# A decoder trunk on one core: unread matmuls at the start, cache pages loaded by fours, the first half's last rows two products sooner

## The chip, the cores and the metric

The kernel runs on one core of one Trainium2 chip. The metric is the device time of one execution in microseconds; a kernel's time is the median of its runs. The kernel before took 1762.97 us (three runs, 1758.93 to 1764.65).

## The reference, cut to what matters

Two layers of a decoder trunk work on 544 tokens: one prompt of 512 and eight samples of four, each sample with 256 tokens of cached past that lie in pages of 128 rows. All is float32. The parts that the change touches:

```python
def rmsnorm(x, g):
    return x * rsqrt(mean(x * x, axis=-1) + 1e-6) * g

h = rmsnorm(x, g_in[l])
z = h @ w_in[l]          # 1024 -> queries, 6 kv streams, gates, conv, pool, ...
# k_cmp, v_cmp (no rotary): rows of the cached pages and of the prompt,
# in overlapping blocks of 32 tokens (stride 16), through a small MLP:
def compress_blocks(rows, pe, w1, w2):
    blk = rows[:, idx] + pe
    return gelu(blk @ w1) @ w2
# compressed attention + top-k selected blocks + sliding window,
# each head's three branches weighted by sigmoid gates (z's 24 gate columns)
...
x = x + merged @ w_out[l]
x = x + ((silu(causal_dwconv3(h2 @ W_a)) * (h2 @ W_b)) @ W_down)   # h2 = rmsnorm(x)
# after the last layer: y = rmsnorm(x, norm_final)
```

## The kernel before

**Products.** Activations lie with features on partitions: eight tiles of 128 x 544, worked in two halves of 272 columns. Weights and activations are split in a high part, rounded to the type that TensorE takes at full rate, and a low part, the rest. A product turns 1024 features into 128: for each of two halves and eight 128-feature slices `mm3` (L321) issues three matmuls, high weights by high activations (L323), high by low (L324) and low by high (L326), 48 in all. A weight tile is loaded by SyncE's queue (SP, L306) as 512 KB into one of three raw buffers; ACT casts it to the high part (L298), DVE subtracts it for the low part (L299), each in two pieces of 128 x 512. The gate product zng has 24 columns; its high and low weights are stacked in one tile (`stacked_weights`: load L313, POOL fill L316, ACT cast L317, DVE subtraction L318).

**Order.** A list of tasks (`tasks`) names the products of a layer. It begins with zkc, zvc, zks (products 0 to 2, run together in the norm group, so that the first layer can start before all of x is normalised), zkw (3), zq0 to zq3 (4 to 7), zvs (8), zvw (9), zng (10), then a convolution product, two pieces of the compression MLP on the key pages, a convolution product, and two pieces on the value pages. `emit` issues a product's matmuls; before that `take` calls `ahead`, which issues weight loads up to three products further on (look=3), and then the task's `pre` is called, if there is one. Within the norm group the `pre` of the second and third product is called just before that product's results are taken out of PSUM. What shall follow a given number of products later is put in a list by `later` and called by `tick` after each product (or, in the last stage, half product).

PE's order is the order of the program. The other engines' instructions are ordered by the framework's scheduler on a simulated timeline, except in the setup, where ACT's and SP's are in program order too. Each engine runs its list in order, and waits on semaphores.

**Pages.** `pages_some` (L450) reads a page's number from a small table into a register of SP (`page`, L443), and issues two loads of 64 KB (L455), one for the key and one for the value rows; they arrive as runs of 256 bytes. 16 pages a layer make 32 loads into two tiles. They are started as `pre` of products: three each ahead of zks, zkw, zq0, zq1 and zq2, and the last one ahead of zq3. `cmp_split` (L525), the `pre` of the first MLP piece, casts the complete tile in eight slices of 128 x 326 (ACT, L532) into one high tile and subtracts (DVE, L534) into eight tiles of the T pool.

The same SP queue carries the weights, the four copies a product that swap halves for the rotary embedding (`z_rope`, L483) and stores of key and value rows (L974).

**Gates.** After zng `nsa_gates` forms the sigmoid gates (L688 to L693); two products later `nsa_rows` transposes them on PE (L700). `v_stack` transposes values on PE (L504), casts them on ACT (L509) and subtracts on DVE (L510) into T tiles; it too is called two products after its own product.

**Start.** `setup` loads x and the first weights in pieces; ACT and DVE form the parts of x (`norm_tile`: L1224 high, L1225 low). PE's first matmul comes when the first weights are cast.

**End.** The last down projection runs half after half: eight output tiles of the first half, then eight of the second, nine matmuls each in the last chunk. After each tile `final_tile` adds it to x and adds its square to a sum. When the first half's eighth tile is done, `final_sum(0)` is put off by fl[0] = 2 products and `final_rows(0)` by fl[1] = 7. `final_sum` sums the squares over partitions by matmuls with ones (L374) and forms the reciprocal root on DVE (L377 to L383); `final_rows` spreads it over partitions by PE transposes (L393), copies it by ACT (L395, L396), multiplies x by it on POOL (L1262, eight tiles for the first half) or DVE (L1264), and stores.

Of the kernel before, what the change touches and what calls it, by code (L numbers as in the profile page):

```python
# [6 lines left out]
F32 = mybir.dt.float32  # L7
F32R = mybir.dt.float32r
# [8 lines left out]
NP = 512  # L17
# [199 lines left out]
class Task:  # L217
    def __init__(self, name, evac, w, x, m, pre, mode, stage, halves, keep):
        self.name, self.evac, self.w, self.x, self.m = name, evac, w, x, m
        self.pre, self.mode, self.stage, self.halves, self.keep = pre, mode, stage, halves, keep  # L220
# [1 line left out]


class Trunk:
    def __init__(self, tc, ins, outs, ctx, slots=49, work=8, fill=1.66, look=3, lag=3, np_=4, nps=2, pm=9, ng=3, raw=3, by_pool=((0, 1, 2, 3, 4, 5, 6, 7), (1, 3, 5)), fl=(2, 7, 6, 1), ys=(4.0, 3.0, 10.0, 3.0, 3.0, 3.5)):
        self.tc, self.nc, self.i, self.o = tc, tc.nc, ins, outs
        pool = lambda name, **k: ctx.enter_context(tc.tile_pool(name=name, **k))
        self.cp = pool("cp", bufs=1)
        self.wp = pool("wp", bufs=4)
        self.bp = pool("bp", bufs=3)  # L230
        self.tp = pool("tp", bufs=slots)
        self.kp = pool("kp", bufs=work)
        self.dp = pool("dp", bufs=1, space=bass.MemoryType.DRAM)
        self.sp = pool("sp", bufs=2)
        self.ps = pool("ps", bufs=1, space=bass.MemoryType.PSUM)
        self.n = 0
        self.ng, self.raw = ng, raw
        self.by_pool, self.fl, self.ys_ = by_pool, fl, ys
        self.np_, self.nps, self.pm = np_, nps, pm
        self.fill, self.look, self.lag = fill, look, lag  # L240


    def nm(self, p):
# [155 lines left out]
    def setup(self):  # L399
        nc, i = self.nc, self.i  # L400
        self.cst = self.cp.tile([128, CS_W], F32, name="cst")
        self.norms = self.cp.tile([128, NM_W], F32, name="norms")
        self.ones = self.cp.tile([128, 2], F32, name="ones")
        self.vc = self.cp.tile([128, 256], F32R, name="vc").rearrange("p (g n) -> p g n", g=2)
        self.cT = self.cp.tile([128, 512], F32R, name="cT")
        self.ptt = self.cp.tile([1, 16], I32, name="ptt")
        self.cst1 = self.cst2 = None
        nc.vector.memset(self.ones, 1.0)
        nc.scalar.activation(self.ones[:, 1:2], self.ones[:, 0:1], AF.Tanh)
        self.x = [self.T() for _ in range(KT)]  # L410
        self.ident = self.c("ident")
        nc.gpsimd.memset(self.vc[64:128].bitcast(F32), 0.0)
        nc.gpsimd.memset(self.cT[64:128].bitcast(F32), 0.0)
        s, v, g = nc.scalar, nc.vector, nc.gpsimd
        by = ((s, None), (s, v), (g, None), (s, v), (s, v), (g, g), (s, v), (s, v))
        ap = self.tl[0].w[0]
        r = self.raw_weights(8)
        for t, a in ((self.norms, i["norms"]), (self.x[0], i["xT"][:, 0]), (r[:, 0:4], ap[:, 0:4]),
                     (self.x[1], i["xT"][:, 1]), (r[:, 4:8], ap[:, 4:8])):
            nc.sync.dma_start(t, a)  # L420
        for k in range(2, 7):
            nc.sync.dma_start(self.x[k], i["xT"][:, k])
        self.norm_tile(0, 0, "g_in")
        w = self.weight_parts(r, 0, 4)
        self.norm_tile(1, 0, "g_in")
        self.got[0] = w + self.weight_parts(r, 4, 8)
        self.nxt = 1
        for k in range(2, 7):
            self.norm_tile(k, 0, "g_in")
        for k in range(3):  # L430
            self.square_sum(self.x[k], k, *by[k])
        self.ahead(2)
        nc.sync.dma_start(self.x[7], i["xT"][:, 7])
        nc.sync.dma_start(self.cst, i["cst"])
        nc.sync.dma_start(self.ptt, i["pt"])
        for u in range(3, 7):
            self.square_sum(self.x[u], u, *by[u])
        self.norm_tile(7, 0, "g_in")
        self.square_sum(self.x[7], 7, *by[7])
# [522 lines left out]
    def tasks(self, l):  # L962
        nc, i = self.nc, self.i
# [3 lines left out]
        def add(name, evac, w, x=h, m=128, pre=None, mode=None, stage="rest", halves=(0, 1), keep=None):  # L967
            T.append(Task(f"{name}.{l}", evac, w, x, m, pre, mode, stage, halves, keep))

        def zt(m):  # L970
            return (i["w_in"][l, m], 8)

        def store(name, j, t):
            nc.sync.dma_start(self.o[name][l, j], t)  # L974
# [28 lines left out]
        def raw_kv(j):  # L1003
            def evac(ps):
                if j == 0:
                    nc.gpsimd.tensor_mul(self.cosr, self.cosr, self.r)
                    nc.gpsimd.tensor_mul(self.sinr, self.sinr, self.r)
                z = self.z_raw(ps)
                store("kvT", j, z)
                self.cmp_prompt(j, z)  # L1010
            return evac

        add("zkc", raw_kv(0), zt(0), pre=begin, mode="norm", stage="z")
        add("zvc", raw_kv(1), zt(1), stage="z")
        pages = lambda a: lambda: self.pages_some(l, range(a, min(a + 3, 16)))

        def rope_k(name, out, j, off, e0):
            def evac(ps):
                z = self.z_rope(ps)
                store(out, j, z)  # L1020
                setattr(self, name, self.k_stack(z, off))
                nc.gpsimd.tensor_copy(self.E[:, :, e0:e0 + 4], self.seq4(z))
            return evac

        add("zks", rope_k("ksel", "kvT", 2, 32, 16), zt(2), pre=pages(0), stage="z")
        add("zkw", rope_k("kwin", "wT", 0, 0, 20), zt(3), pre=pages(3), stage="z")

        def rope_q(r):
            def evac(ps):
                self.q[r] = self.z_rope(ps)  # L1030
                if r == 3:
                    self.sample_prep()
            return evac

        for r in range(4):
            add("zq", rope_q(r), zt(4 + r), pre=pages(6 + 3 * r), stage="z")

        def raw_v(name, out, j, e0):
            def evac(ps):
# [32 lines left out]
        for j in range(2):  # L1072
            for u, nme in enumerate("cxb"):
                add("zconv", conv(j, nme), zt(10 + 3 * j + u), stage="z" if j == 0 and u < 2 else "fill")
                if j == 0 and u < 2:
                    for a in range(2):
                        add("cmp", cmp(u, a), (i["cw1"][l, u][:, 8 * a:8 * a + 8], 8),
                            x=lambda a=a: self.cmpx[8 * a:8 * a + 8],
                            pre=(lambda st=u: self.cmp_split(st)) if a == 0 else None, mode=f"cmp{a}", stage="z")
# [345 lines left out]
```

## Time and profile before

| | us |
|---|---|
| median of three runs (lowest, highest) | 1762.97 (1758.93, 1764.65) |
| the profiled execution | 1759.85 |
| its span, first to last instruction | 1758.0 |
| PE busy | 1710.2 (97%), 13488 matmuls |
| DVE busy | 1145.0 (65%) |
| ACT busy | 737.2 (42%) |
| POOL busy | 487.4 (28%) |

Times in rows are from the start of the span. An engine's busy time is the time in which it executes; in brackets behind a row stands the idle time before it and what ended that. PEclk is the clock granted to PE, 1.00 for 2.4 GHz. A PE record is longer than the pace at which matmuls follow each other, since they overlap. PE at 97% says that a gain can only come from the other 3% or from the clock.

### The profile page before, as it was taken

How to read it: one execution, taken by the hardware profiler on the slowest of the kernel's cores; microseconds unless marked ns; L12 is line 12 of the kernel's file. 1: busy time of each engine (PE TensorE's matmuls, PEld its weight loads, DVE VectorE, ACT ScalarE, POOL GpSimd, SP SyncE). 2: the span in 40 equal slices, each digit the busy share in tenths (PEclk: the TensorE clock that was granted, in tenths of full speed). 3: DMA queues.
4: the chain of work that ended last, by engine and by line, in shares of the span. 5: the costliest groups of instructions: out<-in, count | busy, mean ns of one | idle time of the engine just before them, and what ended most of it. 6: DMA issues, size and time to landing. Idle time of an engine off the chain costs nothing.

```text
span 1758.0 us, 35101 instructions
## 1 busy us (share of the span) xinstructions
PE 1710.2 (97%) x13488; PEld 1689.6 (96%) x13488; DVE 1145.0 (65%) x2552; ACT 737.2 (42%) x1499; POOL 487.4 (28%) x719
## 2 busy tenths in 40 slices
PE   8999989999999999999998998999999999999996
PEld 8999989999999999999998998999999999999996
DVE  6675888856566565565857568887564665565566
ACT  5443555643333233233435345666333333232333
POOL 3212655630122121121231226456001321121113
PEclk9999999999999999999999999999999999999998
DMA  6653211224222322322465532112242222323322
GB/s 216 178 183 113 68 47 46 64 78 150 89 85 74 107 77 86 100 77 77 152 176 148 186 116 49 46 49 64 78 153 90 86 83 91 91 79 97 91 75 78
DMA packets 97208, 175.52 MB, mean 100 GB/s; under 512 B 31250, under 2 KB 51858, under 8 KB 97042
## 3 DMA queue, kind: packets, MB, share of 16 engines
q1 hardware_dynamic: 97042, 173.29, 32.5%
q8 instruction: 107, 1.75, 0.4%
q14 instruction: 59, 0.48, 0.1%
HBM read 157.19 MB, written 12.71 MB: 97 GB/s over the span
## 4 chain that ended last, share of the span: by engine, by line
PE 87%; DVE 7%; SPq 2%; DMA 2%; ACT 1%; issue 1%; POOL 0%; DVEq 0%; ACTq 0%; POOLq 0%
PE pg L323 25%; PE pg L324 25%; PE pg L326 25%; PE ps L830 2%; PE po L910 2%; PE pt L872 2%; SPq L483 1%; SPq L455 1%; DVE mx L846 1%; PE ps L323 1%; PE ps L324 1%; PE ps L326 1%; PE ps L1328 1%; PE ps L1329 1%; PE ps L1330 1%
## 5 line engine op out<-in xcount | busy, mean ns | idle before, releaser
L323 PE MATMUL pg<-t,wh 128*128 128x272 f32 x3824 | 1122.1, 294 | 19.8 <-DVE t L1093 8.3
L324 PE MATMUL pg<-t,wh 128*128 128x272 f32 x3824 | 1104.5, 289 | 0.7 <-DVE t L1225 0.7
L326 PE MATMUL pg<-t,wl 128*128 128x272 f32 x3792 | 1097.3, 289 | 0.0
L323 PEld LDWEIGHTS pg<-t,wh 128*128 128x128 f32 x3824 | 722.7, 189 | 24.6 <-DVE t L1093 8.8
L324 PEld LDWEIGHTS pg<-t,wh 128*128 128x128 f32 x3824 | 723.2, 189 | 2.4 <-DVE t L1225 1.0
L326 PEld LDWEIGHTS pg<-t,wl 128*128 128x128 f32 x3792 | 718.1, 189 | 0.2 <-DVE wl L299 0.2
L298 ACT CAST wh<-wr 128x512 fp32r<-128x512 f32 (+2 forms) x528 | 316.8, 602 | 581.8 <-PE pg L324 464.1
L299 DVE TENSOR_TENSOR wl<-wr,wh 128x512 fp32r<-128x512 f32 (+2 forms) x432 | 299.9, 696 | 164.8 <-ACT wh L298 146.3
L1139 DVE TENSOR_TENSOR t<-t,pg 128x272 f32<-128x272 f32 x204 | 89.1, 437 | 99.4 <-PE pg L326 97.6
L1176 POOL TENSOR_TENSOR W<-W,W 128x512 f32<-128x512 f32 x44 | 78.1, 1776 | 229.6 <-ACT wh L298 200.7
L299 POOL TENSOR_TENSOR wl<-wr,wh 128x512 fp32r<-128x512 f32 (+1 forms) x96 | 114.7, 1197 | 70.1 <-ACT wh L298 64.0
L616 POOL COPY t<-W 128x2 f32<-128x2 f32 x44 | 9.9, 225 | 369.6 <-DVE W L1159 333.0
L859 POOL TENSOR_SCALAR P<-P,ls,gate 128x128 f32<-128x128 f32 (+3 forms) x128 | 79.9, 625 | 95.7 <-DVE ls L857 61.4
L852 ACT ACTIVATE P<-ps,mx 128x256 f32<-128x256 f32 (+1 forms) x144 | 71.4, 498 | 45.7 <-DVE mx L846 33.2
L342 DVE TENSOR_TENSOR t<-W,t 128x544 fp32r<-128x544 f32 x48 | 34.9, 727 | 81.2 <-ACT t L341 81.1
L363 POOL TENSOR_TENSOR t<-t,W 128x544 f32<-128x544 f32 x19 | 26.6, 1399 | 207.4 <-ACT W L354 207.4
L874 ACT CAST b<-pt 128x128 fp32r<-128x128 f32 (+3 forms) x128 | 54.0, 422 | 49.7 <-PE pt L872 49.0
L875 DVE TENSOR_TENSOR b<-pt,b 128x128 fp32r<-128x128 f32 (+3 forms) x128 | 62.0, 485 | 16.6 <-ACT b L874 14.9
L830 PE MATMUL ps<-t,Q 128*128 128x288 f32 (+6 forms) x288 | 64.0, 312 | 4.7 <-ACT P L852 3.6
L341 ACT CAST t<-W 128x544 fp32r<-128x544 f32 x48 | 31.1, 647 | 87.0 <-POOL W L1177 82.5
L846 DVE TENSOR_REDUCE mx<-ps 128x1 f32<-128x256 f32 (+1 forms) x144 | 64.5, 448 | 2.3
L1166 ACT ACTIVATE W<-W 128x560 f32<-128x560 f32 x44 | 29.6, 673 | 74.8 <-DVE W L606 74.8
(254 smaller groups left out, 1833.5 us busy)
## 6 DMA issues: line engine op xcount, KB each, us to landing
wr<-up SPq DMA_DIRECT2D x88, 512.0 KB, 3.6
wr<-w_in SPq DMA_DIRECT2D x83, 512.0 KB, 3.8
wr<-down SPq DMA_DIRECT2D x64, 256.0 KB, 2.7
wr<-w_out SPq DMA_DIRECT2D x16, 512.0 KB, 3.6
wr<-down SPq DMA_DIRECT2D x32, 192.0 KB, 2.4
t<-xT SPq DMA_DIRECT2D x16, 272.0 KB, 5.7
b<-pgA SPq DMA_DIRECT2D x64, 64.0 KB, 2.7
wr<-cw SPq DMA_DIRECT2D x8, 512.0 KB, 3.7
```

The source lines that it names most:

```text
L298: nc.scalar.copy(h, r[:, k0:k1])
L299: (eng or nc.vector).tensor_sub(w, r[:, k0:k1], h)
L323: self.nc.tensor.matmul(p[:m, :HF], wh, xh[:, cs], start=a, stop=False)
L324: self.nc.tensor.matmul(p[:m, :HF], wh, xl[:, cs], start=False, stop=b and wl is None)
L326: self.nc.tensor.matmul(p[:m, :HF], wl, xh[:, cs], start=False, stop=b)
L830: nc.tensor.matmul(p[:, :n], q[:, 128 * i:128 * i + 128], kd[:, c0:c0 + n], start=u == 0, stop=u == 1)
L846: nc.vector.tensor_reduce(mx[:, u:u + 1], p[:, c0:c0 + m], axis=AX.X, op=OP.max, negate=True)
L852: nc.scalar.activation(t[:, pos:pos + m], p[:, c0:c0 + m], AF.Exp, bias=mx[:, 0:1], accum_out=ls[:, u:u + 1])
L859: nc.gpsimd.tensor_scalar(t[:, 0:n], t[:, 0:n], ls[:, 0:1], self.gate[:, i, 1 + kk, hd:hd + 1], op0=OP.mult, op1=OP.mult)
L875: nc.vector.tensor_sub(blk(pt)[:, lo][:, ::-1], blk(p)[:, 0:i + 1], blk(pt)[:, hi])
L1139: self.halves(ps, lambda p, cs: nc.vector.tensor_add(self.x[m][:, cs], self.x[m][:, cs], p))
L1176: nc.gpsimd.tensor_mul(f[:, 0:NP], t[:, 0:NP], z[:, 0:NP])
```

## The change

Three parts. (1) In the setup a work tile is filled with ones by DVE, and ten matmuls of 128 x 512 on it go to a PSUM bank that nobody reads. (2) The pages are started by fours: 0 to 3 as the `pre` of zvc, 4 to 7 of zks, 8 to 11 of zkw, 12 to 15 of zq0; zq1 to zq3 have none. In the norm group, zvc's pages are issued between the work on zkc's and on zvc's results. (3) fl[1] is 5 in place of 7: `final_rows(0)` follows the second half's product m=4 in place of m=6.

```diff
-    def __init__(..., fl=(2, 7, 6, 1), ys=(4.0, 3.0, 10.0, 3.0, 3.0, 3.5)):
+    def __init__(..., fl=(2, 5, 6, 1), warm=10, ys=(4.0, 3.0, 10.0, 3.0, 3.0, 3.5)):
...
         self.ident = self.c("ident")
+        warm = self.W(NP, F32R)
+        nc.vector.memset(warm.bitcast(F32), 1.0)
+        p = self.PT()
+        for _ in range(self.warm):
+            nc.tensor.matmul(p, warm[:, 0:128], warm, start=True, stop=True)
         nc.gpsimd.memset(self.vc[64:128].bitcast(F32), 0.0)
...
-        add("zvc", raw_kv(1), zt(1), stage="z")
-        pages = lambda a: lambda: self.pages_some(l, range(a, min(a + 3, 16)))
+        pages = lambda a: lambda: self.pages_some(l, range(a, a + 4))
+
+        add("zvc", raw_kv(1), zt(1), pre=pages(0), stage="z")
...
-        add("zks", rope_k("ksel", "kvT", 2, 32, 16), zt(2), pre=pages(0), stage="z")
-        add("zkw", rope_k("kwin", "wT", 0, 0, 20), zt(3), pre=pages(3), stage="z")
+        add("zks", rope_k("ksel", "kvT", 2, 32, 16), zt(2), pre=pages(4), stage="z")
+        add("zkw", rope_k("kwin", "wT", 0, 0, 20), zt(3), pre=pages(8), stage="z")
...
         for r in range(4):
-            add("zq", rope_q(r), zt(4 + r), pre=pages(6 + 3 * r), stage="z")
+            add("zq", rope_q(r), zt(4 + r), pre=pages(12) if r == 0 else None, stage="z")
```

## Rows read from the trace of the kernel before

**Rows 1.** Table by stretch: window, length, busy us (instructions) by engine, PEclk, DMA.
```profile
core 0: us, PE busy (x) PEld busy (x) DVE busy (x) ACT busy (x) POOL busy (x), PEclk, DMA share, GB/s
31.00:73.00 42.00, 42.00 (x339) 42.00 (x338) 24.51 (x33) 16.98 (x33) 16.26 (x26) 1.00 0.58 153
5.98:15.70 9.72, 9.02 (x37) 8.47 (x38) 9.03 (x10) 9.03 (x15) 5.13 (x4) 1.00 0.92 358
91.00:94.00 3.00, 3.00 (x13) 3.00 (x12) 3.00 (x8) 3.00 (x6) 0.00 (x0) 0.50 0.27 74
...
897.60:939.60 42.00, 42.00 (x338) 42.00 (x337) 23.64 (x33) 19.07 (x36) 17.75 (x27) 1.00 0.64 161
955.00:958.00 3.00, 2.77 (x21) 2.74 (x22) 3.00 (x9) 3.00 (x5) 0.00 (x0) 1.00 0.00 0
```

**Rows 2.** PE's waits: reader, released by; us in total, times, longest.
```profile
PE pg L323 <- ACT wh L298: 6.0, 1, 6.0
PE pt L700 <- DVE W L693: 5.8, 2, 3.3
...
PE pg L323 <- DVE wh L318: 3.8, 2, 2.0
```

**Rows 3.** ACT's instructions, layer 0 then layer 1: start, length, line, count, idle before.
```profile
62.02 1.15 ACT L298 CAST wh<-wr 128x512 fp32r<-128x512 f32 x2 [2.86 <-DMA wr<-w_in]
...
71.09 2.95 ACT L532 CAST b<-b 128x326 fp32r<-128x326 f32 x4 [7.36 <-DMA b<-pgA]
...
935.50 5.92 ACT L532 CAST b<-b 128x326 fp32r<-128x326 f32 x8 [4.77 <-DMA b<-pgA]
```

**Rows 4.** SP's queue in layer 0: start and length of a run of issues.
```profile
22.12 2.87 SPq L306 DMA_DIRECT2D wr<-w_in  x2
...
31.18 2.75 SPq L455 DMA_DIRECT2D b<-pgA  x5
...
43.27 0.53 SPq L306 DMA_DIRECT2D wr<-w_in  x1
...
50.98 0.58 SPq L306 DMA_DIRECT2D wr<-w_in  x1
51.75 3.72 SPq L455 DMA_DIRECT2D b<-pgA  x6
...
59.42 4.41 SPq L455 DMA_DIRECT2D b<-pgA  x6
```

**Rows 5.** SP's queue in layer 1.
```profile
918.46 0.58 SPq L306 DMA_DIRECT2D wr<-w_in  x1
919.24 3.23 SPq L455 DMA_DIRECT2D b<-pgA  x6
...
925.80 3.58 SPq L455 DMA_DIRECT2D b<-pgA  x6
...
933.30 0.94 SPq L455 DMA_DIRECT2D b<-pgA  x2
```

**Rows 6.** DVE's low parts of the pages, layer 0 and layer 1.
```profile
82.99 4.83 DVE L534 TENSOR_TENSOR t<-b,b 128x326 fp32r<-128x326 f32 x7
...
948.86 4.99 DVE L534 TENSOR_TENSOR t<-b,b 128x326 fp32r<-128x326 f32 x7
```

**Rows 7.** DMA issues: count, KB each, median us from issue to landing.
```profile
wr<-w_in SPq DMA_DIRECT2D x83, 512.0 KB, 3.8
...
b<-pgA SPq DMA_DIRECT2D x64, 64.0 KB, 2.7
```

**Rows 8.** The start: DVE's low parts of weights, PE's first reader of one.
```profile
15.48 1.28 DVE L299 TENSOR_TENSOR wl<-wr,wh 128x512 fp32r<-128x512 f32 x2
...
16.71 0.29 PE L326 MATMUL ps<-t,wl 128*128 128x272 f32 x1
```

**Rows 9.** The end: PE, DVE and POOL around the first half's last rows.
```profile
1739.58 0.49 PE L393 MATMUL po<-cst,ny 128*128 128x128 f32 x3
...
1737.89 0.15 DVE L383 SCALAR_TENSOR_TENSOR ny<-nt,ny 128x3 f32<-128x3 f32 x1
...
1740.75 6.17 POOL L1262 TENSOR_TENSOR W<-t,W 128x272 f32<-128x272 f32 x8 [5.49 <-ACT W L396]
```

More of the change, by code (lines that the diff above doesn't have):

```diff
@@ L224, with __init__ @@
 class Trunk:
-    def __init__(self, tc, ins, outs, ctx, slots=49, work=8, fill=1.66, look=3, lag=3, np_=4, nps=2, pm=9, ng=3, raw=3, by_pool=((0, 1, 2, 3, 4, 5, 6, 7), (1, 3, 5)), fl=(2, 7, 6, 1), ys=(4.0, 3.0, 10.0, 3.0, 3.0, 3.5)):
+    def __init__(self, tc, ins, outs, ctx, slots=49, work=8, fill=1.66, look=3, lag=3, np_=4, nps=2, pm=9, ng=3, raw=3, by_pool=((0, 1, 2, 3, 4, 5, 6, 7), (1, 3, 5)), fl=(2, 5, 6, 1), warm=10, ys=(4.0, 3.0, 10.0, 3.0, 3.0, 3.5)):
         self.tc, self.nc, self.i, self.o = tc, tc.nc, ins, outs
@@ L239, in __init__ @@
         self.np_, self.nps, self.pm = np_, nps, pm
-        self.fill, self.look, self.lag = fill, look, lag
+        self.fill, self.look, self.lag, self.warm = fill, look, lag, warm
     def nm(self, p):
```

## The prediction

> **What bounds the kernel now.** I read four views: the table by stretch, the list of what TensorE (PE) waits for, the DMA issues of SyncE's (SP's) queue, and ACT's and DVE's rows around the waits. The table shows PE busy for 42.00 of 42.00 us in the projection stretch of either layer, with 339 and 338 matmuls in the records, 0.124 us each [rows 1]. A product is 48 of them, 6.0 us, so the stretch holds seven: zkw, zq0 to zq3, zvs, zvw. In layer 0 they begin at 31.0, so zvs begins at 61.0; in layer 1 at 897.6, so zvs begins at 927.6. PE is the bound, and a change gains only what PE waits or runs slowly for. Of its waits the change can touch three [rows 2]: 6.0 for the first cast of weights; 3.8 in two waits for the gate weights' split (L318, before zng); 5.8 in two for L693, which the gate rows' transposes read (L700), 3.3 and so 2.5. Behind the 3.3 the granted clock of 91 to 94 is 0.50, the lower level of 1.2 GHz; behind the 2.5, from 955 to 958, it is 1.00 [rows 1]. Three us at half speed lose 1.5.
>
> **Pages: what they gain.** Why is L318 late? In layer 0 ACT's page casts (L532) wait 7.36 us until 71.09 for the last pages; four take 2.95, and the cast of zng's weights stands behind them. In layer 1 all eight stand in front (5.92 from 935.50) [rows 3]. Of the last pages three are issued from 59.42 in layer 0, and the very last at 933.30 in layer 1 [rows 4, 5]. With four pages ahead of each of products 1 to 4, the last follow zq0's take of weights instead of zq3's, and land about 8 us sooner. The casts are then over before zng's weights come, and the 3.8 goes: -3.8 (bounds -3.8 and 0).
>
> The 5.8 is another matter. DVE makes the eight low parts (L534) just before L693: seven take 4.83 in layer 0 and 4.99 in layer 1, then come L510, the eighth and L693. In layer 1 these subtractions begin at 948.86, seven us after their casts ended at 941.4 [rows 3, 6]. So the pages are not what they wait for; they stand in the T pool behind v_stack's tiles, whose place the change leaves. I keep that order. Layer 0 then looks like layer 1: 3.3 becomes 2.5, -0.8 (bounds -5.8, if they move to the front, and 0).
>
> **Pages: what they push back.** The same queue carries the weights. At look=3 the weights of zvs (product 8) are taken in front of product 5. Up to there the queue now has 9 pages, afterwards all 16: seven more, 14 DMAs. The register loads of page numbers count too: in layer 0 the last ones stand between the page DMAs, which is why six of these take 4.41 and not 3.72 [rows 4].
> Layer 0: zvs's weights are issued at 50.98. The 14 DMAs cost 3.72 + 4.41 (twelve, [rows 4]) + 0.94 (the last two, as in layer 1, [rows 5]), and two loads outside such groups another 0.7, which is what 4.41 has above 3.72 for the two inside: 9.8. Issue 60.8, landing 3.8 later [rows 7], cast 0.57 (1.15 for two, [rows 3]): 65.2, against 61.0. Late by 4.2.
> Layer 1: 3.23 + 3.58 + 0.94 = 7.75 on 918.46 [rows 5] gives 926.2; with 3.8 and 0.57, 930.6 against 927.6. Late by 3.0.
> The low part is 0.64 more (1.28 for two, [rows 8]), and two matmuls of 0.124 go before its first reader: 0.4 for each layer. Together 4.2 + 3.0 + 0.8 = +8.0. Both ends: at the smallest pace in the rows, 0.94 for two, 14 DMAs take 6.6, and the lateness is 1.0 and 1.9, +3.7 with the low parts; at 4.41 for six in both layers 10.3, so 4.7 and 5.6, +11.1. I take the rows of the very DMAs that are moved.
> The weights of zq3 (product 7) move behind six more pages too. Issued at 43.27 today [rows 4], 7.4 later (3.72 for six) and cast by 55.1, they meet a product that begins at 55.0: I put them at 0 (up to 0.6 late in layer 0). Zvw's and zng's weights move behind four pages and one, inside the lateness that zvs already has. The z_rope copies (L483) go up to 9 us later; their readers, the heads, start after this stretch: 0.
> ACT: the page casts are ready from about the time at which zvs's weights land, so one or more can go ahead of their cast. One takes 0.74 (2.95 for four). I count one and a third over both layers, +1.0 (0 to 11.8, all eight in both).
> Clock: layer 0's stall of some 4 us is longer than the 3.3 that was followed by 0.50, so -1.5 at 91 and +1.5 at 65 cancel; layer 1's 3.0 to 3.4 lies between 2.5 (no loss) and 3.3 (loss). 0, bounds -1.5 and +1.5.
>
> **Unread matmuls.** Ten of 512 columns follow a DVE fill, in the 5.98 us in which PE has no weights. At the 0.24 us that a 272-column matmul takes there, (9.72 - 0.70) / 37 [rows 1], ten need some 4.6; a fill of 128x512 should cost no more than a two-operand pass of that size, 0.64 [rows 8]. They fit; if not, the first product starts up to 0.5 late. The gain would be the upper clock from the first product on: the column prints 1.00 for this stretch, but the pace, 0.24 against 0.124, is the lower level's. DVE bounds it: its low parts of the next weights end at about 16.1 and 16.8, and PE, at half pace, reaches the first reader of such a low part (L326 into ps) at 16.71 [rows 8]. So at most 0.6: I take -0.5 (bounds -0.6 and +0.5).
> The Trainium skill (TensorE: Matmul & The Clock Gate, Part 1) says that the array is throttled by default, that activity releases it, and that the point of release differs from run to run. The pace here agrees as to the default; whether ten matmuls release it no run shows. By the rule the term is -0.5, by the rows, in which almost ten us of real matmuls were needed, 0.
>
> **The last rows.** PE's L393 of the first half ran at 1739.58. Two products of nine matmuls (1.1 each) earlier is 1737.3; its ny is ready at 1738.04. So PE waits 0.7 there (it was hidden). In return POOL's eight L1262, 6.17 from 1740.75 to 1746.9 [rows 9], begin 1.5 earlier and leave DVE's short chain for the second half sooner, which shares the stretch with them. I take a gain of 1.1 less the 0.7: -0.4 (bounds -1.5 if the whole move arrives at the end, +0.9 if only the wait does).
>
> **The sum.** +8.0 - 3.8 - 0.8 + 1.0 + 0 - 0.5 - 0.4 = +3.5. Against the profiled execution (1759.85, of which 1758.0 is the span and 1.85 lies around it, unchanged) that is 1763.4. That execution lies 3.1 below the median of the three runs, within their spread; I stay with it: 1763.
>
> **Rivals.**
> A. *The weights are not held up.* The scheduler can issue a load ahead of older pages when its buffer is free: of the two loads at 22.12 to 24.99 the second is zq2's, taken in front of zkw, and it went before pages of zks that stand at 31.18 and come earlier in the program [rows 4]. Against: zq3's, zvs's and zvw's loads each stand at their place in the program. Then the +8.0 and the +1.0 are gone: -3.8 - 0.8 - 0.5 - 0.4 = -5.5, 1754; if the low parts move forward as well, another -5.0 and -1.5 of clock, 1748. Middle 1751.
> B. *Slower: ACT takes the page casts first.* Its place is the cast of zvs's weights, L298. The pages' last landing, 2.7 after their issue [rows 7], comes about 1 us before the weights' 3.8, so the casts can be ready first. With four in front, as layer 0 has them in front of zng's today [rows 3], each layer loses 2.95: 1763.4 - 1.0 + 5.9 = 1768, and layer 1's stall passes 3.3 and costs 1.5 of clock: 1770. With all eight in front, 5.92 a layer: 1776. It decides where more than three go ahead in both layers.
> C. *Both old waits go and the late weights stay*, because L534's tiles come free sooner: 1763.4 - 5.0 = 1758.
> D. *The unread matmuls do not lift the clock*: +0.5, inside the forecast.
>
> **Chances.** The forecast (with D) 0.46, its own range 1759 to 1768; A 0.28; B 0.18; C 0.08. About 0.3%, 5.3 us, is what a measurement of this kernel tells from no change: faster means under 1757.7, slower over 1768.3. Faster: A and half of C, 0.32. Slower: B and the upper edge of the forecast, 0.21. Same: 0.47. The range takes A to its lower third and B to four casts with the clock: 1750 to 1771.
>
> **What would show it.** Right: in the list of PE's waits L318 is gone, and L323 waits for wh of zvs in both layers, about 4 and 3 us; in the queue's rows all 32 page DMAs of a layer stand ahead of zvs's load; L700 still waits about 2.5 twice; the clock is 1.00 at 91. A is right if zvs's load stands before the last pages. B is right if rows of L532 stand between that load's landing and its L298. The start is right if matmul pace is 0.124 from the first product and ps begins at about 16.0; the tail if L1262 begins near 1.5 sooner, counted from the last product. The forecast is wrong if PE does not wait ahead of zvs.

## The result, and the profile after

The changed kernel takes 1774.49 us (median of five runs, 1773.88 to 1775.68) against 1762.97 before (five runs, 1758.1 to 1764.65): the ratio is 1.0074, with a 95% interval of 1.0059 to 1.0088. It is slower, and lies above the forecast's range of 1750 to 1771. The profiled execution took 1774.35 with a span of 1772.5, 14.5 us more than the profiled execution before, which lay 3.1 below its median; the medians differ by 11.5.

Where does the time go? The list of what PE waits for, after:

```profile
PE pg L323 <- ACT W L486: 12.1, 5, 3.7
PE pg L323 <- DVE t L1099: 8.3, 2, 4.1
PE pt L705 <- DVE W L698: 4.6, 2, 2.3
```

Against [rows 2], the wait for zng's split (L318) is gone, that for the gates (L693, now L698) is 4.6 in place of 5.8, and the first wait for weights is gone from the top. New is the first row, 12.1 us in five waits. Its releaser, L486, is `z_rope`'s copy of a product out of PSUM into the W tile (L481 before). PE waits there not for data but for a bank of PSUM, the memory that matmuls write to: the kernel keeps three banks for products, and ACT has not emptied one.

The table by stretch for the two projection stretches, and for the stretch behind each of four of these waits and behind the last gate wait:

```profile
30.18:86.00 55.82, 48.00 (x348) 47.34 (x348) 29.16 (x40) 22.82 (x43) 20.98 (x30) 0.91 0.55 151
48.20:52.20 4.00, 3.97 (x20) 3.97 (x21) 0.36 (x1) 0.26 (x1) 0.25 (x1) 0.59 0.69 171
67.10:72.10 5.00, 4.95 (x22) 4.95 (x23) 4.65 (x6) 4.62 (x9) 1.93 (x1) 0.50 0.64 183
...
903.00:955.00 52.00, 47.72 (x356) 47.28 (x355) 29.34 (x40) 23.15 (x44) 21.57 (x30) 0.93 0.58 152
921.40:925.40 4.00, 3.93 (x22) 3.93 (x23) 0.40 (x1) 0.31 (x2) 0.00 (x0) 0.66 0.53 151
932.00:936.00 4.00, 4.00 (x24) 4.00 (x23) 0.74 (x2) 4.00 (x6) 1.35 (x1) 0.62 0.64 162
...
967.40:973.00 5.60, 5.60 (x24) 5.54 (x25) 5.60 (x12) 5.60 (x9) 0.00 (x0) 0.50 0.30 94
```

In [rows 1] PE worked 42.00 of 42.00 at clock 1.00 in this stretch; now it stands for some 8 us of the first (55.82 less 48.00), and behind the waits the granted clock is 0.50 to 0.66: 20 to 24 matmuls in 4 us (22 in 5 us behind the third wait), where the full pace of 0.124 gives 32 in 4 us. Matching the same matmuls of both traces gives the account of the 14.5, after less before: -0.8 at the start; +12.7 in layer 0's projection stretch, of which 7.8 are the waits of 2.96, 1.15 and 3.71 and 4.9 the slow clock behind them; -4.6 for L318 and the gate rows of layer 0 with its clock; -0.7 up to layer 1; +7.9 in layer 1's stretch, 4.3 in two waits and 3.6 in the clock; -2.4 for its two old waits; +2.9 for the clock behind its gate wait (967.40 to 973.00 at 0.50); -0.5 at the end.

What held ACT up? PE's three waits in layer 0, and ACT's rows from zq0 on:

```profile
48.23 0.39 PE L323 MATMUL pg<-t,wh 128*128 128x272 f32 x1 [2.96 <-ACT W L486]
...
57.18 0.39 PE L323 MATMUL pg<-t,wh 128*128 128x272 f32 x1 [1.15 <-ACT W L486]
...
67.15 0.60 PE L323 MATMUL pg<-t,wh 128*128 128x272 f32 x1 [3.71 <-ACT W L486]
```

```profile
46.51 1.26 ACT L500 CAST t<-t 64x512 fp32r<-64x512 f32 x2 [3.71 <-DVE t L491]
47.79 0.67 ACT L486 COPY W<-pg 128x272 f32<-128x272 f32 x2
54.42 1.15 ACT L298 CAST wh<-wr 128x512 fp32r<-128x512 f32 x2 [5.96 <-DMA wr<-w_in]
55.47 1.25 ACT L500 CAST t<-t 64x512 fp32r<-64x512 f32 x2
56.75 0.68 ACT L486 COPY W<-pg 128x272 f32<-128x272 f32 x2
61.06 5.76 ACT L537 CAST b<-b 128x326 fp32r<-128x326 f32 x8 [3.64 <-DMA b<-pgA]
66.73 0.65 ACT L486 COPY W<-pg 128x272 f32<-128x272 f32 x2
```

Each row of L486 is a copy that PE waits for, at 48.23, 57.18 and 67.15. Ahead of each stands something that waited for a late DMA: the casts of the key rows (`k_stack`, L500) for the rotary rows of zks; the cast of zq3's weights; the eight casts of the pages, which then take 5.76 us themselves. ACT runs its list in order, and stood idle in between. The SP queue shows why these were late:

```profile
35.24 4.90 SPq L460 DMA_DIRECT2D b<-pgA  x8
40.24 2.53 SPq L488 DMA_DIRECT2D W<-W  x4
42.98 4.36 SPq L460 DMA_DIRECT2D b<-pgA  x8
...
50.41 0.58 SPq L306 DMA_DIRECT2D wr<-w_in  x1
...
61.96 0.57 SPq L306 DMA_DIRECT2D wr<-w_in  x1
```

Beside [rows 4]: zq3's weights are issued at 50.41 (43.27 before), zvs's at 61.96 (50.98; the forecast said 60.8), zks's rotary copies at 40.24 (34.03 before). The queue was busy already: before, SP's instructions took 33.9 of the 40.9 us from 31.18 on. Landing explains little of it: over the whole execution it takes 2.1 us for a page and 3.7 for weights, against 2.7 and 3.8 [rows 7]; in the two stretches alone a page takes 2.1 against 2.7, and the two to four loads of weights 4.1 and 4.8 against 3.9 and 4.0.

### The profile page after: what moved, and what is told of

Read it like the earlier page. It is cut to its first block, busy times and chain, and to the rows that moved or that the text cites. A ratio compares the mean times of both kernels' runs of the same rounds, so it can differ in the third digit from the quotient of the medians.

```text
span 1772.5 us, 35106 instructions
## 1 busy us (share of the span) xinstructions
PE 1720.6 (97%) x13498; PEld 1697.4 (96%) x13498; DVE 1147.3 (65%) x2553; ACT 737.0 (42%) x1499; POOL 491.5 (28%) x719
## 4 chain that ended last, share of the span: by engine, by line
PE 88%; DVE 6%; SPq 2%; issue 1%; ACT 1%; DMA 1%; POOL 0%; DVEq 0%; ACTq 0%; POOLq 0%
PE pg L323 25%; PE pg L324 25%; PE pg L326 25%; PE ps L835 2%; PE po L915 2%; PE pt L877 2%; SPq L460 1%; PE ps L1334 1%; DVE mx L851 1%; PE ps L1335 1%; PE ps L1336 1%; PE ps L324 1%; PE ps L323 1%; PE ps L326 1%; PE pt L901 0%
## 5 line engine op out<-in xcount | busy, mean ns | idle before, releaser
L323 PE MATMUL pg<-t,wh 128*128 128x272 f32 x3824 | 1122.3, 294 | 22.7 <-ACT W L486 12.1
L299 DVE TENSOR_TENSOR wl<-wr,wh 128x512 fp32r<-128x512 f32 (+2 forms) x432 | 301.2, 699 | 175.9 <-ACT wh L298 157.3
L299 POOL TENSOR_TENSOR wl<-wr,wh 128x512 fp32r<-128x512 f32 (+1 forms) x96 | 114.9, 1199 | 68.8 <-ACT wh L298 63.0
```

The lines of the kernel that those rows point to most:

```text
L299: (eng or nc.vector).tensor_sub(w, r[:, k0:k1], h)
L323: self.nc.tensor.matmul(p[:m, :HF], wh, xh[:, cs], start=a, stop=False)
```

## The experiments

Theory P: the loss is in ACT's in-order list, in which casts that wait for late DMAs stand ahead of the copies that free PSUM. Rivals: W, the weights of PE's own next product are late (my forecast); U, the unread matmuls or the end carry part of it; D, the pages crowd the DMA engines. All ratios are against the kernel before on the same chip.

**Old pages (e1) and pages alone (e2).** One puts the pages back where they were, the other leaves out the unread matmuls and the new place of the last rows.

```diff
e1: -    pages by fours from zvc      +    pages by threes from zks
e2: -    fl=(2, 5, 6, 1), warm=10     +    fl=(2, 7, 6, 1), no fill and no unread matmuls
```

> The changed kernel with the pages again by threes in front of zks to zq3; the unread matmuls and the earlier last rows stay. Theory P (all of the loss is in the pages: ACT's list stands on page casts, on casts of late rotary rows and of late weights, and so empties PSUM late): 1.3 us faster than the kernel before (0.8 at the start, 0.5 at the end), no PE wait for the rotary copy L486, and the two old waits (L318 about 3.8, the gate rows about 5.8) are back. Rival W (the weights of zvs come late): the same. Rival U (the unread matmuls or the tail carry part of the loss): slower than the kernel before.

> The kernel before with the pages by fours alone. P and W: the whole loss and the 1.3 us of the other two parts on top, +13 to +16 us against the kernel before, with five PE waits for the rotary copy L486 of about 12 us in all. U: clearly less than the changed kernel's loss.

e1: 1.0001 (0.9991 to 1.0012), with one wait of 1.0 for the copy in place of the five (none was expected), L318 at 3.3 and the gate rows at 5.7. e2: 1.0055 (1.0033 to 1.0076), which is 9.7 us (5.8 to 13.4) and not the 13 to 16 that were expected, with 11.8 us of waits for the copy:

```profile
PE pg L323 <- ACT W L481: 11.8, 6, 3.5
```

So the pages carry all of the loss that can be told from nothing, and U falls: by e1's interval the two other parts together cost at most 2.1 us. That interval allows the 1.3 us of gain that were expected, but does not show them.

**Rotary copies on ACT's queue (e3).**

```diff
-            nc.sync.dma_start(s[a:a + 32], z[b:b + 32])
+            nc.scalar.dma_start(s[a:a + 32], z[b:b + 32])
```

> The changed kernel, but the four half-swapping copies of each rotary product are issued by ACT's own queue right behind ACT's copy out of PSUM, so they no longer stand behind the pages on SP's queue. P: the casts of the key rows on ACT no longer wait for late rotary rows, so the first wait of each layer (3.0 and 2.2 us, in zq1) goes with its slow-clock stretch of about 2 us; zq3's weights come up to 5 us sooner on SP's shorter list, so the second (1.2 and 2.1) shrinks or goes; the wait behind the eight page casts (3.7 in layer 0) stays; ACT issues 24 copies a layer. In sum 5 to 10 us faster than the changed kernel. W: the first wait of each layer stays, as no weights are late there; at most 4 us faster. Rival D (the pages crowd the DMA engines, and everything lands late): no change.

1.0031 (1.0021 to 1.0042), some 7.6 us less than the changed kernel, within P's 5 to 10. Every wait for the copy is gone: the first ones, as P had it and W not, but also the one behind the page casts, which P had expected to stay. PE now waits for weights, at zq3:

```profile
PE pg L323 <- ACT wh L298: 5.2, 3, 2.4
...
PE pg L326 <- DVE wl L299: 4.4, 3, 2.2
```

**Casts moved to POOL: the pages' (e4) or the key rows' (e5).**

```diff
e4: -            nc.scalar.copy(hi[:, c], cb[:, :, c::8])
    +            nc.gpsimd.tensor_copy(hi[:, c], cb[:, :, c::8])
e5: -            nc.scalar.copy(k[a, off:], kr[a, 0:NP])
    +            nc.gpsimd.tensor_copy(k[a, off:], kr[a, 0:NP])
```

> The changed kernel, but the eight high parts of the pages are cast by POOL instead of ACT. P: the third wait of layer 0 (3.7 us in zq3, behind eight casts of 5.8 us on ACT) goes with the slow clock of 68 to 72; the first two waits of each layer stay; 4 to 6 us faster than the changed kernel, if POOL's casts are done before the compression needs them. W and D: no change, since neither weights nor DMAs move.

> The changed kernel, but the casts of the key rows (k_stack, two of 0.63 us per key product) are made by POOL instead of ACT; the DMAs stay as they are. P, link by link: ACT no longer stands on late rotary rows, so it empties zq0's PSUM in time and the first wait of each layer (3.0 and 2.2 us) goes, with its slow clock; the second (1.2 and 2.1), behind the cast of zq3's late weights, and the third, behind the page casts, stay or grow by a part of what was saved, since the weights do not come sooner. 3 to 8 us faster than the changed kernel. W (zvs's late weights): no change. D (crowded DMA engines): no change.

e4: 1.0053 (1.0034 to 1.0073); e5: 1.0052 (1.0035 to 1.0070). The intervals overlap that of the changed kernel, so by time neither gain is shown. By place P was right, by size not: in e4 the third wait is gone, but the first two in layer 0 are 3.4 and 2.7 (3.0 and 1.2); in e5 the first is gone in both layers, and the second is 4.9 and 4.7. What stands ahead of it in e5, from ACT's rows:

```profile
55.37 1.14 ACT L298 CAST wh<-wr 128x512 fp32r<-128x512 f32 x2 [11.30 <-DMA wr<-w_in]
56.41 0.66 ACT L486 COPY W<-pg 128x272 f32<-128x272 f32 x2
```

ACT stood 11.3 us for zq3's weights, and two copies of zq1, needed at 51.9, stood behind it. One late thing taken away, the next late thing holds the same list.

**Other doses (e6, e7).** Groups of four from zks, and of three from zvc.

```diff
e6: pre of zvc, zks, zkw, zq0, zq1:      none, pages 0-3, 4-7, 8-11, 12-15
e7: pre of zvc, zks, zkw, zq0, zq1, zq2: pages 0-2, 3-5, 6-8, 9-11, 12-14, 15
```

> The changed kernel with the same groups of four, one product later: ahead of zks, zkw, zq0 and zq1, none ahead of zvc. In front of zks's rotary copies then stand 7 page DMAs of the layer (15 in the changed kernel, 5 before), in front of zq3's weights 15 (23, 11). P: no wait for rotary copies or weights in the first two places; the page casts may still stand in front of one PSUM copy; the L318 wait stays away. Within 4 us of the kernel before. W: zvs's weights stand behind 23 instead of 31 page DMAs, their lateness of 3 to 4 us goes too, and so W cannot be told from P here by the sum, only by the places. U: no faster than the changed kernel.

> The changed kernel with groups of three from zvc on (zvc to zq1 three each, zq2 one). In front of zks's rotary copies stand 11 page DMAs (15, 5), in front of zq3's weights 17 (23, 11), zvs's 23 (31, 17). P: between the changed kernel and the one before: the first wait of each layer 0 to 1 us instead of 3.0 and 2.2, the second mostly gone, the third up to 4 in layer 0: 0 to 6 us slower than before. W: as fast as the kernel before less the two L318 waits, about -4.

e6: 1.0018 (1.0007 to 1.0030), with 9.6 us of waits for the copy; e7: 1.0013 (0.9999 to 1.0027), with 8.7. In sum both are where P put them, between the two kernels. By place the first wait is gone in both, since zks's copies stand behind 7 and 11 page DMAs, but the second, behind zq3's weights, stays (2.1 and 4.2 in layer 0), where I had expected it to go. D falls with e3, which moves the same bytes and is faster, and with the landing times above: the changed kernel's pages land no slower than before, and its weights at most 0.8 us slower, where they are issued 7 and 11 us later.

**The two old waits alone (e8).** The kernel before, with zng's cast on POOL and the gate rows a product later.

```diff
-        nc.scalar.copy(w[:, :, 0:24], r)
+        nc.gpsimd.tensor_copy(w[:, :, 0:24], r)
...
-            self.later(2, lambda: self.nsa_rows(z))
+            self.later(3, lambda: self.nsa_rows(z))
-            self.later(3, self.nsa_sample)
+            self.later(4, self.nsa_sample)
```

> The kernel before (its pages, no unread matmuls, its last rows), with the two old waits taken on directly: zng's high weights are cast by POOL, not by ACT behind the page casts, and the gate rows' transposes (and what follows them) come one product later on PE. If the two waits are what the pages' move was after, this shows what they are worth: -3.8 for L318, -2 to -5.8 for the gate rows (PE may wait for the pages' low parts instead, which DVE makes in the same stretch), -1.5 for the clock behind it: 6 to 10 us faster than the kernel before. If those waits only move: no change.

0.9995 (0.9984 to 1.0007): no change, which was to be seen if those waits only move. Both waits are gone and two others stand in their stead, 4.2 us at L712 (the sample gates' matmuls, which follow the gate rows) and 2.3 at L504 (for DVE's L475).

**ACT's list cleared (e9), and a part of that (e10).** In e9 ACT keeps only the copies in this stretch: the changes of e4 and e5, and the high parts of the weights of zkw to zvw on DVE; in e10 the weights only.

```diff
-        nc.scalar.copy(h, r[:, k0:k1])
+        nc.vector.tensor_copy(h, r[:, k0:k1]) if self.hi_dve else nc.scalar.copy(h, r[:, k0:k1])
```

> The changed kernel with everything that can stand waiting on late DMAs taken off ACT's list in this stretch: the key rows' casts (L500) and the page casts (L537) on POOL, the high parts of the weights of zkw, zq, zvs and zvw on DVE. ACT keeps the copies out of PSUM. The DMAs and their order stay. P (what costs is ACT's list, whose waiting casts hold up the PSUM copies): all PE waits for the copy L486, 12 us, go; what is left is the true lateness of weights, up to 5 us for zvs in layer 0 and 3.5 in layer 1. 8 to 11 us faster than the changed kernel. W (PE waits because its own product's weights are late, and the releaser named is wrong): no gain. D (crowded DMA engines): no gain.

> The changed kernel with only the high parts of those weights moved from ACT to DVE. P: the second wait of each layer (1.2 and 2.1 us, ACT's copies behind the cast of zq3's weights, which waits 6 to 7 us for its DMA) goes; the first (3.0 and 2.2, behind the key rows) and the third (behind the page casts) stay. 2 to 6 us faster than the changed kernel. W: no change.

e9: 1.0078 (1.0056 to 1.0099), not faster than the changed kernel at all; e10: 1.0089 (1.0068 to 1.0110). P predicted 8 to 11 us of gain in e9, and falls as the whole story. The waits show what it missed:

```profile
PE pg L326 <- DVE wl L299: 7.8, 5, 3.3
PE pg L323 <- DVE wh L298: 5.7, 3, 2.7
```

No wait for the copy L486 is left, so the way over ACT's list is real. But the same time comes back as late weights: at zq3 2.7 and 1.4 us, at zvs 1.6 and 3.3, in layer 1 1.4, 1.5 and 1.5. SP issues zvs's weights in this run no sooner than in the changed kernel. Part of the wait for their low parts is DVE's own order: a multiplication (L489) stands between the casts and the subtractions.

```profile
62.83 0.57 SPq L306 DMA_DIRECT2D wr<-w_in  x1
```

```profile
67.77 1.90 DVE L298 CAST wh<-wr 128x512 fp32r<-128x512 f32 x2 [5.08 <-DMA wr<-w_in]
69.59 1.85 DVE L489 TENSOR_TENSOR t<-W,t 128x544 f32<-128x544 f32 x1
71.36 1.28 DVE L299 TENSOR_TENSOR wl<-wr,wh 128x512 fp32r<-128x512 f32 x2
```

In e10 the second wait is gone in layer 0, as P had it, but not in layer 1 (2.3 us), the first of layer 0 is longer (4.2), and DVE, now with the weights' casts in its list, adds 3.3 more; the 2 to 6 us that P expected are not there.

**The clear list with fewer early pages (e11), and with the old ones (e12).**

```diff
e11: the pages of e7, ACT's list as in e9
e12: the pages of the kernel before, ACT's list as in e9
```

> Pages by threes from zvc on, with ACT's list cleared as in the run above. zvs's weights stand behind 23 page DMAs, some 3.5 us later than before, which is inside their room of 5.6 and 4.7 us. P: no PE wait for L486 and none for weights; the L318 wait (3.8) is gone; 2 to 5 us faster than the kernel before. W: as the run of threes alone, 2 slower than before.

> The pages as before the change, the unread matmuls and the earlier last rows, and ACT's list cleared as above. With the page casts on POOL, zng's cast on ACT no longer stands behind them: the L318 wait (3.8) shrinks or goes although no page comes sooner. P: 2 to 5 us faster than the kernel before. If the early pages themselves were needed for that: no faster than the kernel before.

e11: 1.0059 (1.0036 to 1.0081); e12: 1.0025 (1.0013 to 1.0036). Both expectations are wrong: moving casts costs. In e11 ACT's Q activations (L820) wait 11.58 us for the rotary sums and hold the copies (7.0), and POOL's page casts hold zng's fill (L318, 6.4); in e12 L318 is 5.4 in one wait and the gate rows 8.1. Lists in order on DVE and POOL do to PE what ACT's did.

**The queue with half the DMAs (e13, e14).** So I formed theory S: SP's queue is the one cause, and ACT's list only one of its ways to PE; its rival A holds that ACT's list suffices. Only the key half of each page is needed by the first compression product; the value half is needed some products later. e13 issues the key halves at the very places of the change, the value halves behind them; e14 the same a product or more later. The page's number stays in its register.

```diff
+        keys = lambda a: lambda: self.pages_some(l, range(a, a + 4), (0,))
+        vals = lambda a: lambda: self.pages_some(l, range(a, a + 4), (1,))
e13: pre of zvc, zks, zkw, zq0: keys(0), (4), (8), (12); zq1, zq2, zq3, zvs: vals(0), (4), (8), (12)
e14: pre of zks, zkw, zq0, zq1: keys(0), (4), (8), (12); zq2, zq3, zvs, zvw: vals(0), (4), (8), (12)
```

> The kernel before (no unread matmuls) with the earlier last rows, and the 16 key loads of the pages at the very places of the change (by fours ahead of zvc, zks, zkw, zq0); the 16 value loads, which are needed some 10 products later, follow by fours ahead of zq1, zq2, zq3 and zvs, from the page numbers already in registers. In front of zks's rotary copies stand 8 page DMAs (15 in the changed kernel, 5 before), in front of zq3's weights 12 (23, 11), of zvs's 16 (31, 17). S (what costs is SP's queue: every page DMA of 0.57 us in front of rotary copies and weights): no PE wait for weights, at most 1 us for the copy out of PSUM in either layer, L318 gone: 3 to 6 us faster than the kernel before. A (ACT's list alone, whatever the queue does): the page casts stand as early on ACT's list as in the changed kernel, so the waits for PSUM stay: 4 or more slower than the kernel before.

> The same with both groups one product later or more: keys by fours ahead of zks, zkw, zq0, zq1, values ahead of zq2, zq3, zvs, zvw. At each place fewer page DMAs stand in front than in the kernel before (zks's copies 4 for 5, zq3's weights 8 for 11, zvs's 12 for 17). S: no new waits, L318 gone: 3 to 6 us faster than the kernel before. A: page casts in front of one PSUM copy, 2 us slower to 2 us faster.

e13: 1.0001 (0.9991 to 1.0011); e14: 0.9995 (0.9987 to 1.0004). The loss is gone in both. In e13 S holds over A: ACT's page casts stand at least as early on its list as in the changed kernel, two ahead of one copy and six ahead of the next, and PE's waits for the copy are 0.6 us in one.

```profile
PE pt L702 <- DVE W L695: 7.1, 2, 4.8
...
PE pg L323 <- DVE W L691: 1.3, 1, 1.3
...
PE pg L323 <- ACT W L483: 0.6, 1, 0.6
```

```profile
51.00 1.58 ACT L534 CAST b<-b 128x326 fp32r<-128x326 f32 x2 [1.84 <-DMA W<-W]
52.48 0.38 ACT L483 COPY W<-pg 128x272 f32<-128x272 f32 x1
52.76 4.59 ACT L534 CAST b<-b 128x326 fp32r<-128x326 f32 x6
57.26 0.38 ACT L483 COPY W<-pg 128x272 f32<-128x272 f32 x1
```

```profile
42.80 0.52 SPq L306 DMA_DIRECT2D wr<-w_in  x1
...
51.69 0.58 SPq L306 DMA_DIRECT2D wr<-w_in  x1
```

zq3's and zvs's weights are issued at 42.80 and 51.69, within 0.7 us of [rows 4].

e14 does not fit S by place. A copy wait of 3.0 us is left in layer 0, and the rows ahead of that copy hold no idle time: the eight page casts, Q activations and weights' casts follow each other (ACT had stood 3.5 us for a rotary sum shortly before them).

```profile
55.91 6.09 ACT L534 CAST b<-b 128x326 fp32r<-128x326 f32 x8
62.01 1.28 ACT L817 ACTIVATE Q<-t 64x512 fp32r<-64x512 f32 x2
63.31 1.14 ACT L298 CAST wh<-wr 128x512 fp32r<-128x512 f32 x2
64.36 0.38 ACT L483 COPY W<-pg 128x272 f32<-128x272 f32 x1
```

That is what A forecast there, page casts in front of one copy, at the 2 us slower to 2 us faster that A gave. The scheduler makes another list for ACT in every kernel (before, layer 0's page casts [rows 3] come behind all four queries' copies, the last of them at 63.07; in the changed kernel they come ahead of zq2's), and no run held that list fixed while the DMAs moved. So the queue is shown as the cause of late rotary rows and weights; how much of the third wait is the late pages and how much the casts' place on ACT's list stays open.

The gain of 3 to 6 that S promised is not there either. L318's wait is gone, but in e13 the gate rows wait 7.1 and the gates' own sum (L691) 1.3 in place of the 5.8 of [rows 2], and in e14 the copy takes 3.0. Other waits take what the early pages give.

**That wait taken away as well (e15, e16).** The gates' last step stands behind eight low parts of the pages on DVE; POOL makes these instead, in e13's kernel (e15) and in the kernel before with the earlier last rows (e16).

```diff
-            nc.vector.tensor_sub(t, cb[:, :, c::8], hi[:, c])
+            nc.gpsimd.tensor_sub(t, cb[:, :, c::8], hi[:, c])
```

> The keys-then-values kernel with the keys at the places of the change, and the 16 low parts of the pages a layer (L536) subtracted by POOL instead of DVE, so that the gates' last step no longer stands behind eight of them. If DVE's order is what ends the gate rows' wait (7.1 us in that kernel, 5.8 before the change), that wait goes; PE may wait up to 3 us a layer for POOL's slower low parts in the compression. 3 to 8 us faster than the kernel before. If the early pages were worth nothing in any case: no change.

> The kernel before with the earlier last rows and the same move of the low parts to POOL; its pages are as before. The gate rows' wait (5.8) shrinks, the L318 wait (3.8) stays: 1 to 5 us faster than the kernel before, and 2 to 5 slower than the run above, which is what early key pages are worth once nothing else stands behind them.

e15: 0.9979 (0.9966 to 0.9992), medians 1760.21 against 1763.52: faster than the kernel before, by 3.7 us (1.4 to 6.0), at the low end of what was expected. e16: 0.9991 (0.9981 to 1.0001), not told from no change. In both the gate rows' wait is out of PE's list, and in e16 nothing of its size stands in its place, so DVE's order had caused it. The difference between the two is within their intervals, so the worth of early key pages alone, 2 to 5 expected, stays open. e15's runs spread widely, from 1752.33 to 1766.66. Its profiled execution is the slowest, so the profile does not show where the gain comes from; it even has new waits, one of 6.1 us at 88.4 for an earlier step of the same gates (L691) and 5.1 in two for low parts of weights (L299).

## Why the prediction was wrong

**The step that failed** is the sentence "The z_rope copies (L483) go up to 9 us later; their readers, the heads, start after this stretch: 0." Not all readers are the heads. `k_stack`'s casts read the rotary keys, and stand on ACT's list ahead of the copies out of PSUM; zks's copies came 6.2 later (34.03 to 40.24), and the first wait of each layer (3.0 and 2.2) came of it. e5 and e9 showed it: without those casts on ACT this wait is gone. PE waited 5.2 us for it, and ran at the lower clock behind both waits, where the sum had 0. I had looked for what is behind a waiting instruction on SP, and not on ACT. The prediction's own sign of being wrong came with it: in the changed kernel PE does not wait ahead of zvs.

**The weights of zq3**, "I put them at 0": the load came 7.1 later (7.4 forecast), but it does not only meet its product. Its cast waits on ACT's list (5.96 and 6.93 us in the two layers) ahead of zq1's copies. That is the second wait (1.2 and 2.1). In e9, with ACT clear, the product itself still waits 4.1 in layer 0.

**The weights of zvs**, +8.0. Right by mechanism, wrong by what PE saw: the queue pushed them back 11.0 us (9.8 forecast), and e9, with ACT's list clear, waits 4.9 and 3.0 for them (4.6 and 3.4 forecast). That the sizes agree so well is luck: in e9 PE comes to zvs 5.8 us later than at the forecast's 61.0, the load is issued 2.0 later than at its 60.8, and 1.85 of the 4.9 is DVE's multiplication. In the changed kernel PE has lost more than that before it reaches zvs, and no wait for these weights is left.

**The page casts**, +1.0 and rival B. B named the right instructions, eight casts on ACT ahead of something needed, and the right side, but the wrong victim: the copies of zq2 (3.7 us in layer 0), not zvs's weights. Its prices of 1770 to 1776 hold the result by luck, through a sum of other parts.

**The clock**, "0, bounds -1.5 and +1.5": measured about +8.5 in the two stretches and +2.9 behind layer 1's gate wait. I had allowed for one wait beyond 3.3 us; there were five new ones, from 1.2 to 3.7, and four were followed by the lower level.

**What held.** L318 is gone (-3.8 in both). The gate rows' wait stays at 2.3 each (4.6 for 5.0 forecast). The end gained 0.5 (0.4 forecast): POOL's rows of the first half begin 8.8 us ahead of the last transposes and not 7.7, at a price of 0.7 of waiting. From the first matmul of L374 to the end it is 24.2 here against 24.7 before; nine other runs with the earlier rows have 24.2 too, e14 24.4, but e11, e12, e15 and e16 24.8, so the gain does not come in every kernel.

```profile
1753.19 0.51 PE L393 MATMUL po<-cst,ny 128*128 128x128 f32 x3 [0.69 <-DVE ny L383]
...
1763.08 0.87 PE L393 MATMUL po<-cst,ny 128*128 128x128 f32 x3 [2.53 <-DVE ny L383]
```

The unread matmuls do lift the clock: some 1.5 us into the first product matmuls follow each other at 0.12 us in all eleven kernels that have them, and at 0.23 in all seven that do not. What bounds the start is DVE: PE now waits for its normalised parts (L1231), and the first reader of low weights into ps stands at 15.83 here and at 16.09 to 16.72 in the ten others with unread matmuls (mean of the eleven 16.37), against 16.71 before and 16.09 to 17.51 in the six others without (mean of the seven 16.52; 16.35 without e14's 17.51). So the -0.5 is not shown: the 0.9 between this pair of traces does not come back in the others, and 0 to 0.2 is what the runs bear out.

```profile
1.50 3.97 PE L416 MATMUL pt<-W 128*128 128x512 f32 x10 [1.50 <-DVE W L413]
5.95 0.39 PE L323 MATMUL pg<-t,wh 128*128 128x272 f32 x1 [0.48 <-ACT wh L298]
...
9.87 0.39 PE L324 MATMUL pg<-t,wh 128*128 128x272 f32 x1 [1.08 <-DVE t L1231]
```

Ten matmuls sufficed, and without them the full pace begins between 10 and 11 us in e13 and only after 15.7 in e14. In e3, e4 and e10 the clock fell again between 10 and 15 us, after pauses in which PE waited for DVE. The rule weighed in the prediction, that activity releases the clock and that the point of release differs (the Trainium skill, TensorE: Matmul & The Clock Gate, Part 1), agrees with these rows.

**In one sentence:** the change puts up to 14 more page DMAs of some 0.6 us (eight take 4.36 to 4.90) in front of everything else on SP's queue, which delays rotary rows, weights and casts at once; each reaches PE by its own way, and taking one away shows the next. e1 shows that the pages are the cause, and e13 that it is their number on the queue: with half the DMAs at the same places one wait of 0.6 us is left of the three. That the casts' place on ACT's list can cost by itself is what e14's 3.0 points to; its share in the changed kernel stays open.

## What to carry to other kernels

When transfers are moved forward on a busy queue, list all that stands behind them, and for each late arrival not only its reader, but what is behind that reader on its engine's list; PSUM copies on an engine that also waits for DMAs are the first to look at. If a removed stall comes back elsewhere at the same size, look upstream for what both share, and halve its load before moving work between engines. Load early only what is needed early: here that took the loss away, while what it gains stays open.

## What was not expected of the hardware

The length of a wait does not tell what the clock does after it. Before, a wait of 2.5 us was followed by 1.00 [rows 1]; in the changed kernel waits of 2.17 and 2.27 us were followed by 0.66 and 0.50, while the 2.31 ahead of 98.06 was followed by 1.00:

```profile
98.00:101.50 3.50, 3.44 (x25) 3.40 (x26) 3.50 (x9) 3.50 (x6) 0.00 (x0) 1.00 0.02 7
```

A DVE subtraction that otherwise takes 0.67 took 4.80 while POOL worked through eight subtractions in a row (e15, layer 0, DVE's row and POOL's); PE waited 6.1 us behind it. In layer 1 of the same run one beside POOL's eight took 1.42, and in e16 those beside POOL's eight (11.34 us in a row, layer 0) took 0.67 to 0.98. What makes the difference was not tried.

```profile
81.92 4.80 DVE L299 TENSOR_TENSOR wl<-wr,wh 128x512 fp32r<-128x512 f32 x1 [4.26 <-ACT wh L298]
```

```profile
77.97 8.20 POOL L536 TENSOR_TENSOR t<-b,b 128x326 fp32r<-128x326 f32 x8
```
